# Hymba trunk layer: each pair's filled-in projections moved from ahead of the bonus products to ahead of the keys' transposes

## Chip, cores and metric

The kernel runs on one core of a Trainium2 chip. Its time is that of the device for one execution, in microseconds (us), and the median of several runs counts; lower is better. The core has a matrix engine (PE, whose weight loads the profile lists apart as PEld), a vector engine (DVE), a scalar engine (ACT), GpSimd (POOL) and a sync engine (SP) that issues most DMAs. Each works through its own instructions in order and waits at semaphores for the others. PE writes its products to PSUM, which has eight banks; ACT or DVE take them from there.

## What is computed

One layer of a hybrid decoder trunk for 512 prompt rows and 32 sample rows (8 requests of 4), all float32. Around the middle stand two half-step SwiGLU feed-forward parts with layer norms; in the middle a RWKV-7 recurrence of 8 heads of 64 runs beside a gated short convolution. Cut to what matters:

```python
x = layer_norm(ALPHA * x + 0.5 * swiglu(x, wg, wu, wd), ln1_g, ln1_b)
proj = x @ w_in                                   # r, k, v, decay, a, gate; conv columns
ps_mix = ps + mu_shift * (prev - ps)              # token shift of the RWKV columns
kk = normalize(k * k_k); k = k * (1 + (a - 1) * k_a)
def step(s, inp):                                 # per head, s is 64 x 64
    sa = einsum("bhij,bhj->bhi", s, -kk_t)
    s = s * w_t + sa (kk_t * a_t)^T + v_t k_t^T
    return s, einsum("bhij,bhj->bhi", s, r_t)
o = group_norm(o) + sum(r * k * r_k) * v          # the last term is the bonus
mix = concat(o * g, conv(c_b, c_c, c_h)) @ w_out
x = layer_norm(ALPHA * x + mix, ...); then the second SwiGLU and layer norm
```

## The kernel before, in words

All large weights are split into a high and a low part (`wsplit`: a copy on ACT, L135, and a subtraction on DVE, L136, about 1 us each for 128 x 1024), and each product is three matmuls (`mm3`, L152 to L154). The 544 rows are worked in two halves of 256 and 288 columns; a product of one half has eight input blocks, so 24 matmuls.

The recurrence is done in chunks of 64 steps. The 8 heads make four *pairs* of two; pairs 0 and 1 are group 0, pairs 2 and 3 group 1. The order by time is: scores of pairs 0 and 1 (about 424 to 456 us), elimination of group 0 (`elim`), its rounds, its recurrence and norm, then scores of pairs 2 and 3 (553 to 582), elimination and rounds of group 1, its recurrence, then the output projection and the second feed-forward part.

`Pair.scores` is the critical piece of work here. For one pair it makes:

- three groups of score products (L1057) for the 9 chunks and both heads. They go to five tiles `sm` and one tile `mm`, and DVE multiplies each by a mask into SC (L1060, six masks; the sixth reads the `mm` tile). Two DMAs write SC to DRAM (L1064), from where the elimination loads it.
- two groups of transposes, of chunks 0 to 4 and then 5 to 8: the keys (L1071 and, packed, L1050), which ACT copies to BK and BS (L1080, L1082; for pair 2's first group DVE, L1078), and the values (L1088, L1090, L1091), which ACT copies to UV and UP (L1096, L1099). The operand `bkb` of L1057 and L1071 holds the pair's derived keys.
- the bonus products (L1103, two, of 256 and 320 columns), which DVE multiplies with the values (L1104).

PSUM's eight banks are five tiles named `sm` (scores, transposes, bonus) and three named `mm` (background products and the sixth score tile), taken in turn. A new tile waits until the one that had the bank before has been read.

The background is a queue `bg` of generators: the projections of the next pairs and of the convolution, whose products are cut into *pieces* of six matmuls (two input blocks), which yield 658 for 256 columns and 738 for 288. `weave(key, crit)` runs the critical generator, and at each number that it yields it runs pieces worth that number times `FILL[key]`: 0.93 for pair 0, 1.832 for pair 1, 0.531 for pair 2 and 0.85 for pair 3. At least one piece runs at any number above zero. The last piece of a product yields only 300 or nothing, so that a further piece may follow.

Where the next pairs need it, derivations run on DVE between these: L996, L1027 to L1040 make the next pair's keys, L914 and L918 mix a projection's columns. `elim` (L1122 to L1131) is a chain of small DVE steps; its result goes through DRAM (L1132, L1133) and comes back by L1136 into DM, and the rounds start with L1166 on PE. In the recurrence PE's L1248 waits for L1240 on DVE.

The code gives the order in which work is offered; the scheduler of the language then writes each engine's row of instructions by what it takes to be ready, and can put an instruction ahead of or behind where the code has it. What stands in the rows is shown with the change.

Of the kernel before, what the change touches and what calls it, by code (L numbers as in the profile page):

```python
# [55 lines left out]
def R(par):  # L56
    return slice(64 * par, 64 * par + 64)
# [4 lines left out]
def body(ctx: ExitStack, tc: tile.TileContext, xT, gu1, wd1, win, wo_c, wo_0, wo_1, gu2, wd2, wl, ln3, eye, lora, vec, cst,  # L62
# [27 lines left out]
    def big():  # L90
        return ps.tile([P, 512], F32, name="mm", bufs=3)

    def sm():
        return ps.tile([P, 512], F32, name="sm", bufs=5)
# [795 lines left out]
    def s64(x):  # L890
        return x.rearrange("p (c t) -> p c t", t=64)
# [74 lines left out]
    class Pair:  # L966
# [75 lines left out]
        def scores(self):  # L1042
            p, pl, bkb, nk, vf = self.p, self.pl, self.bkb, self.nk, self.v

            def packed(qs, c0, src):
                for par, q in enumerate(qs):
                    for i, x in enumerate(src(par)):
                        if x is not None:
                            r0 = 64 * par + 32 * i
                            PE.matmul(q[r0:r0 + 32, c0:c0 + 64], x, ident[R(par), :], start=True, stop=True)  # L1050

            AR, bv = ARs[p // 2], bvs[p // 2]
            for a0c, n in ((0, 4), (4, 4), (8, 1)):
                qs = (sm(), sm() if n > 1 else big())
                for c in range(n):
                    for par, q in enumerate(qs):
                        PE.matmul(q[:, c * P:(c + 1) * P], bkb[R(par), a0c + c, par:par + 2, :], AR[R(par), pl, a0c + c, :, :],  # L1057
                                  start=True, stop=True)
                for par, q in enumerate(qs):
                    DVE.tensor_tensor(SC[:, pl, par, a0c:a0c + n, :], q[:, :P * n].rearrange("p (c t) -> p c t", c=n),  # L1060
                                      (msk if n > 1 else msks)[:, None, :].to_broadcast([P, n, P]), op=OP.mult)
                yield 0
            for par in range(2):
                dma(Ad[par].rearrange("(c d) s t -> d s c t", d=2)[pl, 0:64], SC[R(par), pl, par, 0:8, 0:64])  # L1064
            yield 500
            for a0c, n in ((0, 5), (5, 4)):
                qs = (sm(), sm())
                m = n - a0c // 5
                for c in range(m):
                    for par, q in enumerate(qs):  # L1070
                        PE.transpose(q[:, c * 64:(c + 1) * 64],  # L1071
                                     bkb[R(par), a0c + c, par:par + 2, :].rearrange("p s t -> p (s t)"), ident[R(par), :])
                if a0c:
                    packed(qs, 192, lambda par: (bkb[R(par), 8, 2 * par, 0:32], bkb[R(par), 8, 1, 0:32]))
                for par, q in enumerate(qs):
                    src, dst = s64(q[:, :64 * m]), BK[:, pl, par, a0c:a0c + m, :]
                    if p == 2 and not a0c:
                        DVE.tensor_copy(dst, src)  # L1078
                    else:
                        ACT.activation(dst, src, AF.Copy)  # L1080
                    if a0c:
                        ACT.activation(BS[R(par), pl, 64 * par:64 * par + 64], q[R(par), 192:256], AF.Copy)  # L1082
                qs = (sm(), sm())
                for c in range(n):
                    t = 64 * (a0c + c)
                    d = slice(c * 64, (c + 1) * 64)
                    if t:
                        PE.transpose(qs[0][:, d], vf[R(0), t - 64:t + 64], ident[R(0), :])  # L1088
                    else:
                        PE.matmul(qs[0][R(1), d], vf[R(0), t:t + 64], ident[R(0), :], start=True, stop=True)  # L1090
                    PE.transpose(qs[1][R(0), d], vf[R(1), t:t + 64], ident[R(1), :])  # L1091
                if a0c:
                    packed(qs, 256, lambda par: (None, vf[R(par), TP:TP + 32]))
                for par, q in enumerate(qs):
                    o = R(1 - par)
                    ACT.activation(UV[o, pl, par, a0c:a0c + n, :], s64(q[o, :64 * n]), AF.Copy)  # L1096
                    if a0c:
                        v = slice(64 * par + 32, 64 * par + 64)
                        ACT.activation(UP[v, pl, :], q[v, 256:320], AF.Copy)  # L1099
                yield 500  # L1100
            for t0, t1, _ in SEG:
                q = sm()
                PE.matmul(q[:, :t1 - t0], bo, nk[:, t0:t1], start=True, stop=True)  # L1103
                DVE.tensor_tensor(bv[pl][:, t0:t1], vf[:, t0:t1], q[:, :t1 - t0], op=OP.mult)  # L1104
# [664 lines left out]
```

## Time and profile before

| | |
|---|---|
| median of 3 runs | 1072.67 us (1072.48 to 1074.12) |
| the profiled execution | 1072.43 us, span 1070.7 us |
| mean granted clock of PE | 0.998 |
| busy: PE, DVE, ACT, POOL | 98%, 79%, 54%, 14% of the span |
| PE busy in 424 to 445 us | 20.65 of 21 us |
| PE busy in 565 to 582 us | 16.22 of 17 us |

A row of a timeline gives the start, the duration, the engine, the line of the kernel, the operation, what it writes and reads (tile names without numbers), its shape and how many such instructions the row stands for; in brackets how long the engine was idle before it, and which instruction released it. Consecutive matmuls overlap, so the durations of rows add up to more than the time between their starts; lengths are taken from start to start. A row of the view by stretches gives the stretch, its length, the busy time of PE, PEld, DVE, ACT and POOL with the number of instructions, the granted clock, the share of the DMA engines and GB/s. A row of the view of waits gives who waits for whom, with total us, number of times and the longest. A row of the DMA issues gives the number of transfers, the size of one and the median us from issue to landing.

### The profile page before, as it was taken

How to read it: one execution, taken by the hardware profiler on the slowest of the kernel's cores; microseconds unless marked ns; L12 is line 12 of the kernel's file. 1: busy time of each engine (PE TensorE's matmuls, PEld its weight loads, DVE VectorE, ACT ScalarE, POOL GpSimd, SP SyncE). 2: the span in 40 equal slices, each digit the busy share in tenths (PEclk: the TensorE clock that was granted, in tenths of full speed). 3: DMA queues.
4: the chain of work that ended last, by engine and by line, in shares of the span. 5: the costliest groups of instructions: out<-in, count | busy, mean ns of one | idle time of the engine just before them, and what ended most of it. 6: DMA issues, size and time to landing. Idle time of an engine off the chain costs nothing.

```text
span 1070.7 us, 22612 instructions
## 1 busy us (share of the span) xinstructions
PE 1050.7 (98%) x9178; PEld 1010.5 (94%) x9178; DVE 844.7 (79%) x1557; ACT 583.2 (54%) x1070; POOL 154.9 (14%) x273
## 2 busy tenths in 40 slices
PE   9999999999999999999999999999999999999997
PEld 8999999999999999899889988999999999999996
DVE  6797888979875777793578657988979888797757
ACT  5746555555553668654444435767555555555524
POOL 0111121211200022133101200001211212121000
PEclk9999999999999999999999999999999999999999
DMA  8558585676854233324145724434766848668512
GB/s 292 132 112 186 120 199 135 145 172 132 186 118 158 79 88 109 85 82 99 41 143 161 173 81 139 141 119 79 152 165 137 200 101 194 143 137 189 147 43 84
DMA packets 91528, 144.48 MB, mean 135 GB/s; under 512 B 34848, under 2 KB 52384, under 8 KB 91296
## 3 DMA queue, kind: packets, MB, share of 16 engines
q1 hardware_dynamic: 68144, 110.76, 34.2%
q0 software_dynamic: 22848, 31.72, 19.2%
q8 instruction: 72, 1.18, 0.4%
q10 hardware_dynamic: 432, 0.56, 0.2%
q14 instruction: 32, 0.26, 0.1%
HBM read 128.81 MB, written 9.75 MB: 129 GB/s over the span
## 4 chain that ended last, share of the span: by engine, by line
PE 76%; DVE 13%; ACT 7%; issue 2%; DMA 2%; POOL 0%; ACTq 0%; DVEq 0%; SPq 0%
PE mm L553 9%; PE mm L554 9%; PE mm L555 9%; PE sm L553 6%; PE sm L554 6%; PE sm L555 6%; PE mm L152 6%; PE mm L153 5%; PE mm L154 5%; DVE hhl L141 2%; ACT hl L135 2%; DVE hl L136 2%; PE sm L441 1%; PE sm L1166 1%; PE mm L784 1%
## 5 line engine op out<-in xcount | busy, mean ns | idle before, releaser
L136 DVE TENSOR_TENSOR hl<-raw,hl 128x1024 fp32r<-128x1024 f32 (+3 forms) x230 | 270.2, 1179 | 63.7 <-ACT hl L135 62.6
L135 ACT ACTIVATE hl<-raw 128x1024 fp32r<-128x1024 f32 (+3 forms) x230 | 232.9, 1020 | 69.7 <-DVE raw L519 43.5
L152 PE MATMUL mm<-xhl,hl 128*128 128x256 f32 (+1 forms) x704 | 209.2, 299 | 0.5 <-ACT xhl L140 0.5
L153 PE MATMUL mm<-xhl,hl 128*128 128x256 f32 (+1 forms) x704 | 203.0, 289 | 0.4 <-DVE xhl L141 0.4
L154 PE MATMUL mm<-xhl,hl 128*128 128x256 f32 (+1 forms) x704 | 202.0, 287 | 0.0
L152 PEld LDWEIGHTS mm<-xhl,hl 128*128 128x128 f32 x704 | 132.0, 188 | 6.9 <-issue 2.0
L153 PEld LDWEIGHTS mm<-xhl,hl 128*128 128x128 f32 x704 | 132.3, 188 | 2.7 <-issue 1.0
L154 PEld LDWEIGHTS mm<-xhl,hl 128*128 128x128 f32 x704 | 132.3, 188 | 0.3 <-issue 0.2
L555 PE MATMUL sm<-xhl,hl 128*128 128x272 f32 x432 | 125.2, 290 | 0.0
L554 PE MATMUL sm<-xhl,hl 128*128 128x272 f32 x432 | 124.4, 288 | 0.0
L553 PE MATMUL sm<-xhl,hl 128*128 128x272 f32 x432 | 124.1, 287 | 0.0
L553 PE MATMUL mm<-tv,hl 128*128 128x272 f32 x288 | 83.3, 289 | 0.3
L555 PE MATMUL mm<-tv,hl 128*128 128x272 f32 x288 | 83.4, 290 | 0.0
L554 PE MATMUL mm<-tv,hl 128*128 128x272 f32 x288 | 83.1, 288 | 0.0
L553 PEld LDWEIGHTS sm<-xhl,hl 128*128 128x128 f32 x432 | 81.4, 188 | 0.0
L554 PEld LDWEIGHTS sm<-xhl,hl 128*128 128x128 f32 x432 | 81.3, 188 | 0.0
L555 PEld LDWEIGHTS sm<-xhl,hl 128*128 128x128 f32 x432 | 81.2, 188 | 0.0
L532 POOL DMA_DIRECT2D raw<-in_wd x32 | 39.2, 1462 | 288.0 <-DVE hlb L141 225.2
L526 POOL DMA_DIRECT2D raw<-in_gu x36 | 43.3, 1203 | 203.5 <-DVE hlb L141 143.8
L553 PE MATMUL mm<-hhl,hl 128*128 128x272 f32 x192 | 56.4, 300 | 0.3
L554 PE MATMUL mm<-hhl,hl 128*128 128x272 f32 x192 | 55.9, 291 | 0.8 <-DVE hhl L141 0.2
L553 PEld LDWEIGHTS mm<-tv,hl 128*128 128x128 f32 x288 | 54.2, 188 | 1.9 <-ACT cpb L620 1.9
(416 smaller groups left out, 2716.0 us busy)
## 6 DMA issues: line engine op xcount, KB each, us to landing
raw<-in_gu SPq DMA_DIRECT2D x84, 512.0 KB, 4.5
raw<-in_gu POOLq DMA_DIRECT2D x36, 512.0 KB, 6.6
raw<-in_wd SPq DMA_DIRECT2D x32, 512.0 KB, 4.5
raw<-in_win SPq DMA_DIRECT2D x26, 512.0 KB, 3.6
raw<-in_wd POOLq DMA_DIRECT2D x32, 256.0 KB, 6.0
z<-sv POOLq DMA_DIRECT2D x16, 272.0 KB, 8.4
raw<-in_wo_c SPq DMA_DIRECT2D x8, 512.0 KB, 3.6
raw<-in_wd SPq DMA_DIRECT2D x8, 384.0 KB, 3.2
```

Of the source, the lines that this page charges most:

```text
L135: seen["hi"] = ACT.activation(hl[:, 0, a:b], raw[:, a:b], AF.Copy)
L136: seen["lo"] = DVE.tensor_tensor(hl[:, 1, a:b], raw[:, a:b], hl[:, 0, a:b].bitcast(F32), op=OP.subtract)
L141: return DVE.tensor_tensor(lo, x, hi.bitcast(F32), op=OP.subtract)
L152: PE.matmul(out, wh, src[:, 0, k, c0:c1], start=(start and i == 0), stop=False)
L153: PE.matmul(out, wh, src[:, 1, k, c0:c1], start=False, stop=False)
L154: seen["fill"] = PE.matmul(out, wl, src[:, 0, k, c0:c1], start=False, stop=(stop and i == n - 1))
L441: PE.matmul(o[i][h][:, :c1 - c0], block(hl, v, k), xhl[:, y, k, c0:c1], start=(k == 0 and j == 0), stop=(k == KD - 1 and j == 2), skip_gro ...
L526: POOL.dma_start(x.rearrange("p (s c) -> p s c", s=2), bass.AP(tensor=a11.tensor, offset=a11.offset, ap=[[2 * D, P], [P * 2 * D, 2], [1, 5 ...
L532: POOL.dma_start(four(x)[:, i], bass.AP(tensor=a11.tensor, offset=a11.offset, ap=[[DFF, P], [P * DFF, 2], [1, 256]]), accum_op=OP.add)
L553: PE.matmul(out, wh, src(0, i), start=(first and i == 0), stop=False, skip_group_check=True)
L554: PE.matmul(out, wh, src(1, i), start=False, stop=False, skip_group_check=True)
L555: PE.matmul(out, wl, src(0, i), start=False, stop=(i == n - 1), skip_group_check=True)
```

## The change

Two yields of `Pair.scores` get other numbers. The one behind the masks yields 1000 instead of 500, and the one at the end of the second group of transposes 0 instead of 500; the one at the end of the first group stays 500.

```diff
             for par in range(2):
                 dma(Ad[par].rearrange("(c d) s t -> d s c t", d=2)[pl, 0:64], SC[R(par), pl, par, 0:8, 0:64])
-            yield 500
+            yield 1000
             for a0c, n in ((0, 5), (5, 4)):
...
-                yield 500
+                yield 0 if a0c else 500
             for t0, t1, _ in SEG:
                 q = sm()
                 PE.matmul(q[:, :t1 - t0], bo, nk[:, t0:t1], start=True, stop=True)
```

In pieces of background (ahead of the key transposes, between the two groups, ahead of the bonus products): pair 0 has 1, 1, 2 before and 2, 2, 0 after; pair 1 has 2, 2, 2 and 4, 2, 0; pair 2 has 1, 1, 1 and 1, 1, 0; pair 3 has half a piece, 2, 1 and two, 2, 0. What is not run there runs behind the bonus products or has run already.

The first place is PE in pair 0, from the sixth score product (to `mm_5067`) to the first key transpose. Before, with `mm_5035` as the background product:

```order
L1057 MATMUL mm_5067<-AR0_4714,bkb_4806 128x128 [waits Activation_49]
L152 MATMUL mm_5035<-xhl_68,hl_5005 128x288
L153 MATMUL mm_5035<-xhl_68,hl_5005 128x288
L154 MATMUL mm_5035<-xhl_68,hl_5005 128x288
...
L1071 MATMUL sm_5080<-cs_4701,bkb_4806 128x64 [waits DVE_49]
L1071 MATMUL sm_5081<-cs_4701,bkb_4806 128x64 [waits DVE_49]
```

There are six matmuls of `mm_5035` between these. After the change twelve stand there, and ahead of the bonus products, where six of 288 and six of 256 columns stood, now none does; the last rows of the second group of transposes (a packed value block) are followed at once by L1103:

```order
L1088 MATMUL sm_5149<-cs_4701,v_4303 128x64 [waits Pool_49]
L1091 MATMUL sm_5150<-cs_4701,v_4303 64x64
L1050 MATMUL sm_5149<-cs_4701,v_4303 32x64
L1050 MATMUL sm_5150<-cs_4701,v_4303 32x64
L1103 MATMUL sm_5165<-nk_4805,cs_4701 128x256 [waits Activation_49]
L1103 MATMUL sm_5168<-nk_4805,cs_4701 128x320 [waits PE_49,Activation_49]
```

What moved is the background between the last transposes and L1103.

The second place is PE in pair 1, the key transposes of the first group. Before, the ten stand together behind twelve matmuls of `mm_5276`, and the next background, `mm_5368`, follows the values:

```order
L154 MATMUL mm_5276<-xhl_68,hl_5272 128x256
L1071 MATMUL sm_5340<-cs_4701,bkb_5172 128x64 [waits DVE_49]
L1071 MATMUL sm_5341<-cs_4701,bkb_5172 128x64 [waits DVE_49]
...
L1091 MATMUL sm_5355<-cs_4701,v_4303 64x64
L152 MATMUL mm_5368<-xhl_68,hl_5272 128x288 [waits DVE_49]
L153 MATMUL mm_5368<-xhl_68,hl_5272 128x288
```

After the change:

```order
L154 MATMUL mm_5276<-xhl_68,hl_5272 128x256
L1071 MATMUL sm_5353<-cs_4701,bkb_5172 128x64 [waits DVE_49]
L1071 MATMUL sm_5354<-cs_4701,bkb_5172 128x64 [waits DVE_49]
...
L1071 MATMUL sm_5353<-cs_4701,bkb_5172 128x64
L152 MATMUL mm_5340<-xhl_68,hl_5272 128x288 [waits DVE_49]
L153 MATMUL mm_5340<-xhl_68,hl_5272 128x288
...
L154 MATMUL mm_5340<-xhl_68,hl_5272 128x288
L1071 MATMUL sm_5354<-cs_4701,bkb_5172 128x64
L1071 MATMUL sm_5353<-cs_4701,bkb_5172 128x64
```

Twelve matmuls of `mm_5340`, which waits for DVE, now stand behind the fifth of the ten key transposes; the other five, the values and twelve more matmuls of the same product follow. The instruction of DVE that its wait names is the sixth mask, whose tile had the same bank.

The third place is DVE in pair 3, around the six masks. Before:

```order
L918 SCALAR_TENSOR_TENSOR T12_4300<-pb_7002,vc_66,dt_7003 128x32
L136 TENSOR_TENSOR hl_7335<-raw_7334,hl_7335 128x1024 [waits DMAHW7_49,PE_49,Activation_49]
L1060 TENSOR_TENSOR SC_4703<-sm_7031,cs_4701 128x512 [waits PE_49]
L1060 TENSOR_TENSOR SC_4703<-sm_7032,cs_4701 128x512 [waits PE_49]
L1060 TENSOR_TENSOR SC_4703<-sm_7043,cs_4701 128x512 [waits PE_49]
L1060 TENSOR_TENSOR SC_4703<-sm_7044,cs_4701 128x512 [waits PE_49]
```

After the change:

```order
L918 SCALAR_TENSOR_TENSOR T12_4300<-pb_6995,vc_66,dt_6996 128x32
L136 TENSOR_TENSOR hl_7204<-raw_7203,hl_7204 128x1024 [waits DMAHW0_49,PE_49,Activation_49]
L1060 TENSOR_TENSOR SC_4703<-sm_7025,cs_4701 128x512 [waits PE_49]
L1060 TENSOR_TENSOR SC_4703<-sm_7026,cs_4701 128x512 [waits PE_49]
L136 TENSOR_TENSOR hl_7339<-raw_7338,hl_7339 128x1024 [waits DMAHW7_49,Activation_49]
L1060 TENSOR_TENSOR SC_4703<-sm_7037,cs_4701 128x512 [waits PE_49]
L1060 TENSOR_TENSOR SC_4703<-sm_7038,cs_4701 128x512 [waits PE_49]
```

A second split of a weight stands between the second and the third mask. The split that came first before stood earlier, in pair 3's derivation (between L1027 and L1028, at 563.59 us in the profile), and has moved out of it to ahead of the masks. Elsewhere on DVE a few splits, L914 and steps of the eliminations change places.

## The prediction

> **What bounds the kernel now.** I read the first part of the page, to see which engine sets the pace:
>
> ```profile
> span 1070.7 us, 22612 instructions
> ...
> PE 1050.7 (98%) x9178; PEld 1010.5 (94%) x9178; DVE 844.7 (79%) x1557; ACT 583.2 (54%) x1070; POOL 154.9 (14%) x273
> ```
>
> PE is busy for 1050.7 of 1070.7 us, so 20 us in all are PE's idle time. The change takes no matmul away and adds none. It can gain only idle time of PE around the four scores stages, and lose by making new idle time there or in what depends on them. So I asked for PE's waits from the first scores stage to the second output projection (424 to 680 us):
>
> ```profile
> PE sm L1248 <- DVE UV L1240: 3.4, 8, 0.7
> ...
> PE sm L1091 <- DVE SC L1060: 0.8, 3, 0.3
> PE sm L1071 <- DVE SC L1060: 0.7, 2, 0.3
> ```
>
> The columns are total us, times, longest. The longest, 3.4 us, lie in the recurrence behind the scores (L1248). For the masks (L1060 on DVE) PE waits 1.5 us in five places: the key transposes (L1071) and value transposes (L1091) need PSUM banks that the masks still read. That is what more background products ahead of the key transposes can cover. How dense the stage is shows the view by stretches of time, for pair 1:
>
> ```profile
> 445.00:458.00 13.00, 12.20 (x131) 10.69 (x128) 9.22 (x16) 10.62 (x25) 1.55 (x10) 1.00 0.33 73
> ```
>
> PE is busy 12.20 of 13 us at a granted clock of 1.00: 0.8 us idle is all there is to win here.
>
> **Pair 0.** The PE timeline (start, duration, line, count, and in brackets idle time with its releaser):
>
> ```profile
> 427.87 0.40 PE L152 MATMUL mm<-xhl,hl 128*128 128x288 f32 x1
> ...
> 428.86 0.54 PE L1071 MATMUL sm<-cs,bkb 64*128 64x64 f32 x10
> 429.47 0.33 PE L1090 MATMUL sm<-cs,v 64*64 64x64 f32 x2
> 430.07 0.24 PE L1091 MATMUL sm<-cs,v 64*64 64x64 f32 x1 [0.28 <-DVE SC L1060]
> ...
> 430.47 0.40 PE L152 MATMUL mm<-xhl,hl 128*128 128x288 f32 x1
> ...
> 434.26 1.13 PE L1103 MATMUL sm<-nk,cs 128*128 128x256 f32 x4
> ```
>
> One piece of background (six matmuls of 288 columns) takes 428.86 - 427.87 = 0.99 us ahead of the first group of transposes. The group then takes 1.61 us to the next piece, part of it waiting for the fourth mask. After the change two pieces stand ahead, two between the groups and none ahead of the bonus products. I need three lengths that this stage doesn't show undisturbed, and take them from pair 1:
>
> ```profile
> 448.81 0.52 PE L1071 MATMUL sm<-cs,bkb 64*128 64x64 f32 x9 [0.33 <-DVE SC L1060]
> ...
> 450.40 0.40 PE L152 MATMUL mm<-xhl,hl 128*128 128x288 f32 x1
> ...
> 452.19 0.40 PE L1071 MATMUL sm<-cs,bkb 64*128 64x64 f32 x6
> ...
> 453.39 0.40 PE L152 MATMUL mm<-xhl,hl 128*128 128x288 f32 x1
> ...
> 455.08 1.13 PE L1103 MATMUL sm<-nk,cs 128*128 128x256 f32 x4
> ```
>
> Twelve matmuls of 288 columns take 452.19 - 450.40 = 1.79 us up to the transposes; the second group of transposes 453.39 - 452.19 = 1.20 us. Six of 256 with six of 288 take 1.68 (pair 3's rows below, 575.23 to 576.91).
>
> After the change, then: background from 427.87, transposes at 427.87 + 1.79 = 429.66. The fourth mask let L1091 start at 430.07, so almost nothing is left to wait for: ten key transposes are 0.54 busy, and from the first L1091 to the next piece it is 430.47 - 430.07 = 0.40, together 0.94. The next piece starts at 430.60, the second group at 432.28, the bonus products (L1103) at 433.48 instead of 434.26: **0.78 us gained**. If only the marked wait of 0.28 goes, group 1 takes 1.61 - 0.28 = 1.33 and the gain is 0.39; I take 0.78, since the masks are done by then, and keep 0.39 as the other end. Below nothing it can't be, since the masks end when they did and PE has the same work. What follows of pair 0 (the derivation of pair 1's keys on DVE) starts earlier too: the same weight split moves ahead of the first bonus product's L1104 on DVE and costs nothing there, since L1104 waits for L1103.
>
> **Pair 1, the place that costs.** Here a yield is worth more background: two pieces stood ahead of the transposes, and four do now. The scheduler writes the first two of these (mm_5276), then five of the ten key transposes, then the other two pieces (mm_5340), and then the other five transposes. The pieces of mm_5340 write a PSUM bank that the sixth mask still reads. Before the change the same bank was first written by the piece at 450.40, behind all the first group. The sixth mask, on DVE:
>
> ```profile
> 450.06 0.28 DVE L1060 TENSOR_TENSOR SC<-mm,cs 128x128 f32<-128x128 f32 x1
> ```
>
> It ends at 450.34; the piece at 450.40 came 0.06 behind it. With everything 0.78 earlier it ends at 449.56 and the pieces start at 449.62. PE, in order, has nothing else meanwhile: the five transposes and the values, which used to fill this wait, now stand behind the pieces. From there: 1.79 for twelve matmuls, 451.41; five transposes (half of 0.52) with the values (0.40) and the change of operands between them, about 0.75, 452.16; twelve matmuls, 453.95; second group, 455.15 for L1103. Without the change in pair 1 it would be 455.08 - 0.78 = 454.30. So **0.85 us lost**, and pair 1 leaves PE 0.07 late. The ends: if the masks don't come earlier with pair 0 (DVE's chain on its own), the loss counts from 450.34 and the stage ends 0.86 late instead of 0.07. If the pieces need not wait, they start behind the five transposes: the second mask lets these run from 448.81 - 0.78 = 448.03, so the pieces from 448.29, and L1103 comes 1.79 + 0.75 + 1.79 + 1.20 later, at 453.82, a gain of 0.48 on 454.30 instead of a loss.
>
> [...]
>
> **Pairs 2 and 3.** Here a yield is worth one piece. In pair 2 the piece ahead of L1103 moves behind it: bonus products and pair 3's derivation start 0.9 to 1.0 earlier, and nine matmuls of 256 fewer stand ahead of pair 3's score products: 0.133 - (1.79 - 1.68)/6 = 0.115 each, 1.0 us. Pair 3's rows, PE and DVE:
>
> ```profile
> 570.10 2.14 PE L1057 MATMUL sm<-AR,bkb 64*128 64x128 f32 x33
> ...
> 575.23 0.38 PE L152 MATMUL mm<-xhl,hl 128*128 128x256 f32 x1
> ...
> 576.91 0.40 PE L1071 MATMUL sm<-cs,bkb 64*128 64x64 f32 x6
> ...
> 579.01 1.13 PE L1103 MATMUL sm<-nk,cs 128*128 128x256 f32 x4
> ```
>
> ```profile
> 571.16 1.22 DVE L136 TENSOR_TENSOR hl<-raw,hl 128x1024 fp32r<-128x1024 f32 x1
> 572.30 2.68 DVE L1060 TENSOR_TENSOR SC<-sm,cs 128x512 f32<-128x512 f32 x5
> ```
>
> The scores start at about 569.0, so the masks could start 1.1 earlier or more. But between the second and the third mask DVE now makes another weight split, which holds it for 572.30 - 571.16 = 1.14 us. Laid behind one another, DVE's rows put masks one and two about 1.36 earlier (one split less ahead of them, 1.14, and 0.22 that the earlier bonus products bring), three to six only 0.22: the fourth lets L1091 start 0.22 us earlier, and the background behind it starts at 575.01 instead of 575.23. The last piece moves behind L1103 and joins the background there, which saves one start behind small products: the first matmul of a piece costs about 0.1 more than those inside (six take 0.99 alone, twelve 1.79, not 1.98). **0.33 us gained**; ends: nothing (the masks stay where they are) and 0.6 (one PE wait at L1071 and one at L1091 gone, 0.3 each).
>
> **Sum.** -0.78 + 0.85 - 0.33 = -0.26 us. Behind the scores PE is as full as elsewhere, so a shift of PE arrives at the end. The profiled execution took 1072.43 us (span 1070.7 and 1.7 around it), which gives 1072.17. The median of the three runs, 1072.67, is 0.24 above it, and the same difference gives **1072.4**. With all ends on the good side it is -0.78 - 0.48 - 0.6 = -1.86, on the bad side +0.86 (pair 1's masks not earlier, nothing in pair 3). A measurement of this kernel can tell about 0.2%, 2.1 us, from no change; the forecast lies far inside.
>
> **What else hangs on the moved steps.** ACT evacuates the second group later or earlier with PE, and no bank is wanted sooner than it is freed: in pair 0 ACT now takes the copy of a weight split before that group, and by the order of the rows ends it about when the group ends on PE. The masked scores go through DRAM: two loads of DM follow the eliminations of group 1, and the chunk products wait for them:
>
> ```profile
> 597.77 1.32 SPq L1136 DMA_DIRECT2D DM<-Dd  x2
> ```
>
> ```profile
> DM<-Dd SPq DMA_DIRECT2D x2, 256.0 KB, 6.1
> ```
>
> ```profile
> 606.27 2.08 PE L1166 MATMUL sm<-DM,SC 64*64 64x64 f32 x64
> ```
>
> The second load is issued half of 1.32 after 597.77 and lands 6.1 us later, at about 604.5; its first user starts at 606.27, so 1.8 us of lateness are covered. The scheduler writes pair 2's and 3's splits in other places of DVE's row, and I expect the elimination to end up to 0.7 us later and at most one split, 1.22. Both lie below 1.8, so I cost it at nothing. SP's queue passes one weight load behind the two Dd writes, which only helps them. In group 0 the elimination's last steps move ahead of a weight split and of the convolution's work on DVE, so its load can only be earlier.
>
> **Rivals.**
> 1. The pieces of pair 1 don't stall PE, because the sixth mask comes earlier or frees the bank in time. Then pair 1 gains 0.48: -0.78 - 0.48 - 0.33 = -1.59, 1071.1, still within 0.2%. Against it: the mask ended 0.06 before the row at 450.40, and DVE has a split, a scan and the five other masks ahead of it in the same order as now. Chance 0.11.
> 2. Slower: group 1's elimination. The two splits beside pair 3's masks and those moved in the elimination add up, DM lands late, and PE runs out of background ahead of L1166. It decides from 1.8 us of lateness on, each us beyond costs one, and slower by over 0.2% needs 1.8 + 2.1 + 0.3 = 4.2 us, three and a half splits: 1074.8 or so. For it: DVE is busy 79% and in order. Against it: the number of splits in the stretch is the same. Chance 0.13.
> 3. The stall in pair 1 lowers the clock. [...] Nothing in the rows shows a clock below 1.00 here. Chance 0.04.
> 4. The change does nothing: PE's pieces move but each gain is a wait elsewhere, 1072.7. Chance 0.05.
> 5. Faster: DVE's new order in group 0 lets the elimination and the splits end earlier, and of the 3.4 us that PE waits at L1248 two thirds go, because a split or copy no longer stands ahead of L1240: -0.26 - 2.2, 1070.2. For it: the order on DVE does change there. Against it: these waits sit in a chain of PE and DVE that the change leaves as it is. Chance 0.09.
>
> **How the numbers follow.** The forecast, 1070.8 to 1073.5 by its ends, has 0.58. Same is 0.58 + 0.11 + 0.05 = 0.74, faster 0.09 (rival 5), slower 0.17 (rivals 2 and 3). The range goes from 1070.5, short of rival 5, to 1074.6, into rival 2 and short of rival 3; it leaves out 0.04 + 0.09 and a part of rival 2, under 0.2 together.
>
> **What would show it.** Right: in pair 0 no PE wait at L1091, and L1103 about 5.6 us behind the first background matmul (433.48 - 427.87), not 6.4; in pair 1 a wait at L152 of 1 us or more whose releaser is DVE SC L1060, between two rows of five L1071; in pair 3 a split between the second and third mask, and L1091 still released by a mask; PEclk at 9 throughout. Wrong: no wait at L152 in pair 1 (rival 1); a wait at L1166 for DM (rival 2); a clock below 1.00 (rival 3); or PE waits in the recurrence that grow by more than the terms above.

## The result, and the profile after

The changed kernel takes 1075.21 us (median of 17 runs, 1072.77 to 1076.7), the kernel before 1072.54 (17 runs, 1071.69 to 1074.25). The ratio is 1.0018, 95% interval 1.0012 to 1.0025: slower by 1.9 us by the ratio and by 2.7 by the medians, clear of the noise though small. The forecast was that nothing measurable would change, and the time lies outside the stated range of 1070.5 to 1074.6. The profiled execution took 1076.37 us, 3.94 more than that of before.

The page of the changed kernel:

```profile
span 1074.6 us, 22614 instructions
...
PE 1054.8 (98%) x9178; PEld 1014.0 (94%) x9178; DVE 844.2 (79%) x1557; ACT 582.4 (54%) x1070; POOL 154.4 (14%) x273
...
PEclk9999999999999999899999999999999999999999
```

PE is busy 4.1 us longer for the same 9178 matmuls. So on balance the time did not go into waits: the same work ran slower, and one slice of PEclk, the seventeenth (430 to 457 us), shows an 8. The waits of PE between 424 and 680 us:

```profile
PE sm L1248 <- DVE UV L1240: 3.4, 8, 0.7
PE mm L152 <- DVE SC L1060: 1.3, 1, 1.3
PE sm L1239 <- ACT W L1233: 0.9, 3, 0.4
PE sm L1090 <- DVE SC L1060: 0.9, 1, 0.9
```

The second row is the stall that was predicted, a background matmul (L152) that waits for a mask, once, 1.3 us. The fourth is new as well and was not predicted. The recurrence's waits (first row) are what they were. Pair 1 on PE:

```profile
448.45 0.34 PE L1071 MATMUL sm<-cs,bkb 64*128 64x64 f32 x4 [0.33 <-DVE SC L1060]
450.04 0.40 PE L152 MATMUL mm<-xhl,hl 128*128 128x288 f32 x1 [1.25 <-DVE SC L1060]
...
450.67 0.29 PE L153 MATMUL mm<-xhl,hl 128*128 128x288 f32 x1
450.80 0.35 PE L154 MATMUL mm<-xhl,hl 128*128 128x288 f32 x1
450.95 0.44 PE L152 MATMUL mm<-xhl,hl 128*128 128x288 f32 x1
451.19 0.44 PE L153 MATMUL mm<-xhl,hl 128*128 128x288 f32 x1
```

The stall ends at 450.04. The matmuls behind it start 0.13 apart, as before; from 450.95 on they start 0.24 apart and last 0.44 instead of 0.29. In the view by stretches (the column behind POOL's is the granted clock) the clock is lower in just this time:

```profile
450.00:451.00 1.00, 0.96 (x7) 0.96 (x8) 0.38 (x1) 0.00 (x0) 0.56 (x4) 0.95 0.68 179
451.00:457.00 6.00, 6.00 (x35) 5.32 (x34) 1.37 (x2) 1.63 (x4) 0.00 (x0) 0.50 0.36 49
457.00:458.00 1.00, 1.00 (x16) 0.55 (x14) 0.00 (x0) 0.56 (x3) 0.11 (x1) 0.63 0.00 0
```

For 0.10 + 6 + 0.74 = 6.84 us the granted clock is 0.50. That is rival 3 of the prediction, the one with a chance of 0.04.

### The profile page after: what moved, and what is told of

The parts are those of the page before. It is cut to its first block, busy times and chain, and to the rows that moved or that the text cites. A ratio compares the mean times of both kernels' runs of the same rounds, so it can differ in the third digit from the quotient of the medians.

```text
span 1074.6 us, 22614 instructions
## 1 busy us (share of the span) xinstructions
PE 1054.8 (98%) x9178; PEld 1014.0 (94%) x9178; DVE 844.2 (79%) x1557; ACT 582.4 (54%) x1070; POOL 154.4 (14%) x273
## 4 chain that ended last, share of the span: by engine, by line
PE 80%; DVE 11%; ACT 5%; DMA 2%; issue 2%; ACTq 0%; DVEq 0%; SPq 0%
PE mm L553 9%; PE mm L554 9%; PE mm L555 9%; PE mm L152 7%; PE mm L153 6%; PE mm L154 6%; PE sm L553 6%; PE sm L554 6%; PE sm L555 6%; DVE hhl L141 2%; ACT hl L135 2%; PE sm L441 1%; DVE hl L136 1%; PE sm L1166 1%; PE mm L784 1%
## 5 line engine op out<-in xcount | busy, mean ns | idle before, releaser
L152 PE MATMUL mm<-xhl,hl 128*128 128x256 f32 (+1 forms) x704 | 209.9, 300 | 1.8 <-DVE SC L1060 1.3
L152 PEld LDWEIGHTS mm<-xhl,hl 128*128 128x128 f32 x704 | 132.7, 189 | 8.0 <-issue 2.2
```

What stands on the lines that cost most here:

```text
L152: PE.matmul(out, wh, src[:, 0, k, c0:c1], start=(start and i == 0), stop=False)
```

## The experiments

The theory made from this, A: PE's idle time in pair 1 lets the granted clock fall (0.50 for 6.84 us in the profile), and that is most of the loss. The rival, B: the new order itself costs the time (transposes behind four pieces, masks behind a split), and the clock only goes along. A kernel's runs and the runs of before stand on the same chip. Each run gives a mean granted clock, and times of one kernel go with it: of the changed kernel's 17 runs the four at 0.999 took 1072.77 to 1073.69, the eight at 0.995 or 0.996 took 1075.79 to 1076.7. A mean of 0.998 alone does not mean that the clock fell during the work: it also drops behind the last matmul, to 0.50 at 1065.81 us in the profile of the kernel before and at 1072.13 in that of the changed one, and the first of these has 0.998 for that reason alone.

**The change without pair 1.**

```diff
-            yield 1000
+            yield 500 if p == 1 else 1000
...
-                yield 0 if a0c else 500
+                yield 0 if a0c and p != 1 else 500
```

> The change for pairs 0, 2 and 3, with pair 1's two yields as they were before. Theory A (the clock): what cost the time is PE's idle time of 1.25 us in pair 1 behind the fifth key transpose, which lets the granted clock fall to half for some 6.7 us. Without that idle time no row shows a clock below 0.9, pair 0 keeps its gain of 0.3 to 0.8, pairs 2 and 3 come out within 0.3 of nothing, and the time is 1071.6 to 1072.5, a ratio of 0.999 to 1.000 to the kernel before. Theory B (the order): the loss is in the later masks and transposes themselves, in pair 3 as much as in pair 1, and the clock only goes along. Then about half of the loss stays: 1073.5 to 1074.5, ratio 1.001 to 1.002.

Measured: 1072.57 us, ratio 0.9997 (0.9988 to 1.0006), clock in 445 to 462 us 1.00. The loss is gone with pair 1's part, although pair 3's does all it did in the changed kernel (a wait of 0.9 us at L1090 there). A's ratio came in (its time lies 0.07 above A's upper end), B's didn't.

**The change for pair 1 alone.**

```diff
-            yield 500
+            yield 1000 if p == 1 else 500
...
-                yield 500
+                yield 0 if a0c and p == 1 else 500
```

> The change for pair 1 alone; pairs 0, 2 and 3 yield as before. Theory A: the wait for the sixth mask at the first background matmul behind the fifth transpose is there again, 1.2 to 1.6 us, the granted clock falls to half in some runs behind it, and the median is 1075 to 1077, ratio 1.0025 to 1.004, with single runs near 1073.3 in which the clock did not fall or fell for a shorter time. Theory B: pair 1 alone costs the 0.85 us of the prediction's term and no more, 1073.4, ratio 1.001, with little spread.

Measured: 1075.06 us (1073.46 to 1076.89), ratio 1.0020 (1.0011 to 1.0028). Pair 1 alone gives a loss as large as the whole change. A's median came in, its ratio (1.0025 to 1.004) was too high; B's number and its little spread did not come in. The profiled execution of this kernel took 1073.69 us; it shows the same stall without a fall of the clock, which separates the two:

```profile
448.84 0.34 PE L1071 MATMUL sm<-cs,bkb 64*128 64x64 f32 x4 [0.33 <-DVE SC L1060]
450.44 0.41 PE L152 MATMUL mm<-xhl,hl 128*128 128x288 f32 x1 [1.25 <-DVE SC L1060]
...
452.23 0.40 PE L1071 MATMUL sm<-cs,bkb 64*128 64x64 f32 x5
```

```profile
445.00:462.00 17.00, 15.29 (x150) 13.41 (x147) 12.36 (x29) 11.50 (x27) 1.93 (x12) 1.00 0.27 57
```

The wait is 1.25 us in both. Here twelve matmuls take 452.23 - 450.44 = 1.79 us, in the changed kernel's profile 452.52 - 450.04 = 2.48, and the next twelve 3.17 (454.10 to 457.27). From the stall's end to L1103 it is 5.76 here (to 456.20) and 8.62 there (to 458.66): the fall of the clock cost 2.86 us of PE's time. What the stall and its order cost without a fall is worked out below.

**The stall filled with work.** The changed kernel, with pair 1's larger yield in two halves and repeated transposes between them, which write the same values to the first transposes' tiles:

```diff
+            if p == 1:
+                yield 500
+                first = (sm(), sm())
+                for i in range(28):
+                    q = first[i % 2]
+                    PE.transpose(q[:, 0:64], bkb[R(i % 2), 0, i % 2:i % 2 + 2, :]..., ident[R(i % 2), :])
-            yield 1000
+            yield 500 if p == 1 else 1000
             for a0c, n in ((0, 5), (5, 4)):
-                qs = (sm(), sm())
+                qs, first = first or (sm(), sm()), None
```

> The changed kernel, but in pair 1 twenty-eight repeated transposes (the same result written to the first two tiles of the transposes again and again) stand behind the first two pieces of background, where PE waited for the sixth mask; all ten key transposes then follow the background. The wait for the mask is as long as in the changed kernel, but PE works through most of it; the work behind it is 0.26 us longer. Theory A: the clock stays at 1.00 in this stretch and the time falls to 1072.2 to 1073.2, ratio 0.9995 to 1.0006. Theory B: the transposes and the background come as late as in the changed kernel, so the time stays at 1075 to 1076.5.

And the same with `range(10)`:

> As the run with twenty-eight repeated transposes in pair 1, but with ten: PE works for 0.5 us less... about 0.9 us less of the wait for the sixth mask, so that some 1.3 to 1.4 us of idle time is left there, about that of the changed kernel. Theory A with a sharp limit on idle time (the clock falls where PE is idle for over 1.2 us or so within 3.4 us): the clock falls in more than half the runs and the median is 1074.5 to 1076. Theory A with a gradual chance: some runs at 1073 to 1074, some at 1075 and over, median 1074 to 1075. Theory B (no clock): 1073.8 as with twenty-eight, since the work behind the mask is the same.

Measured: with 28 repeats 1073.79 us (1073.03 to 1075.38), ratio 1.0008 (1.0000 to 1.0017); with 10 repeats 1076.41 us (1074.16 to 1083.45), ratio 1.0039 (1.0024 to 1.0054). PE's rows at the stall, with 28:

```profile
448.28 1.09 PE L1071 MATMUL sm<-cs,bkb 64*128 64x64 f32 x27 [0.33 <-DVE SC L1060]
449.88 0.40 PE L152 MATMUL mm<-xhl,hl 128*128 128x288 f32 x1 [0.50 <-DVE SC L1060]
```

With 10:

```profile
448.22 0.52 PE L1071 MATMUL sm<-cs,bkb 64*128 64x64 f32 x9 [0.33 <-DVE SC L1060]
...
449.81 0.40 PE L152 MATMUL mm<-xhl,hl 128*128 128x288 f32 x1 [1.07 <-DVE SC L1060]
```

The two kernels differ in 18 transposes whose result is thrown away. The background starts at the same time within 0.1 us, and the kernel with *more* work for PE is faster by 2.6 us in the median. The two ran on different chips; their ratios to the kernel before, each taken on one chip, differ by 0.0031, some 3.3 us. The clocks of the runs with 28 are 0.997 to 0.999, those with 10 are 0.990 to 0.999. B has no account of that. A's number for 28 repeats was too low by 0.6 us: PE still waits 0.50 for the mask and 0.5 once at L995, for ACT, and neither stands in it. A's two medians for 10 repeats (1074 to 1075 and 1074.5 to 1076) were too low as well. With ten repeats PE has less idle time in pair 1 than in the changed kernel (1.52 us in the worst 3.4, against 1.71), and yet the loss is larger. So the size of the idle time in pair 1 does not by itself set the loss, and that the 18 transposes help by filling this one stall is not shown: the only profile with ten repeats that shows a fall, below, has it at pair 2.

**Second profiles.** The changed kernel once more, and the one with ten repeats once more, no edits:

> The changed kernel once more, for a second profile. If the fall of the clock is a matter of where PE's idle 1.25 us lies against a window that runs on its own, this profile shows either the same wait with the clock at 1.00 and a time of 1073 or so, or the same wait with the clock at 0.5 for some 3.4 or 6.7 us and 1074.7 or 1076.4: steps of about 1.7 us. If the fall belongs to the wait itself, it is the same as in the first profile, 6.7 us.

> The run with ten repeated transposes once more, for a profile. Its times reach from 1074.2 to 1083.5 at mean clocks from 0.999 to 0.990, and the one profile shows no fall. If the spread is the clock's, a profile at 1075.5 or above shows the clock at 0.5 in one or several stretches of about 3.4 us, which begin within 3.4 us behind the waits of pair 1 or pair 3; a profile near 1074.2 shows none. If it were something else, a profile at 1075.5 or more would show the clock at 1.00 and longer waits or loads.

The changed kernel took 1076.01 us, with the clock down in two places:

```profile
450.00:451.00 1.00, 1.00 (x8) 1.00 (x7) 0.00 (x0) 0.00 (x0) 0.21 (x2) 0.60 0.90 195
451.00:453.00 2.00, 2.00 (x14) 1.49 (x13) 1.37 (x2) 0.41 (x2) 0.00 (x0) 0.50 0.16 20
453.00:454.00 1.00, 1.00 (x12) 0.83 (x12) 0.00 (x0) 0.65 (x3) 0.00 (x0) 0.69 1.11 104
...
518.00:519.00 1.00, 1.00 (x11) 0.93 (x8) 0.76 (x4) 0.43 (x2) 0.00 (x0) 0.73 0.00 0
519.00:521.00 2.00, 2.00 (x12) 2.00 (x11) 0.43 (x2) 0.00 (x0) 0.00 (x0) 0.50 0.00 0
521.00:522.00 1.00, 1.00 (x7) 0.78 (x6) 0.00 (x0) 0.00 (x0) 0.00 (x0) 0.56 0.00 0
```

The first is 0.80 + 2 + 0.62 = 3.42 us at half clock behind the stall, the second 0.54 + 2 + 0.88 = 3.42 us in the recurrence of group 0. The first profile's 6.84 is twice that. The kernel with ten repeats took 1079.36 us, and its fall lies at pair 2:

```profile
555.00:559.00 4.00, 2.81 (x37) 2.31 (x37) 3.26 (x6) 1.27 (x3) 0.00 (x0) 1.00 0.38 83
559.00:560.00 1.00, 1.00 (x7) 1.00 (x6) 1.00 (x3) 0.00 (x0) 0.00 (x0) 0.71 0.88 357
560.00:569.00 9.00, 9.00 (x65) 6.90 (x65) 3.98 (x10) 2.92 (x10) 0.00 (x0) 0.50 0.19 46
569.00:570.00 1.00, 1.00 (x8) 1.00 (x8) 0.97 (x2) 0.00 (x0) 0.00 (x0) 0.67 0.00 0
```

0.58 + 9 + 0.66 = 10.24 us, three times 3.41, and the run is 5.2 us above the profile of the same kernel without a fall (1074.16), about half of 10.24. So the falls measured in these three profiles last 3.42, 6.84 and 10.24 us, one, two and three times 3.41, and the same stall is followed by none (pair 1 alone), by 3.42 us or by 6.84. The expectation that a fall begins within 3.4 us behind a wait of pair 1 or 3 failed for that last one, which follows 4 us in which PE is idle for 1.19, in one wait for DVE at pair 2's score products.

The traces also show in what the like stalls differ. The changes of the granted clock named here lie whole numbers of stretches of 3.413 us apart, called windows below and laid in each trace from the first entry of its clock. In the changed kernel this entry is at 7.18 us, and the fall (450.91), the rise (457.74) and the fall behind the last matmul (1072.13) come 130, 132 and 312 windows behind it; in the kernel before it is at 4.27, and the one fall, at 1065.81, comes 311 windows behind it. In the second profile of the changed kernel the falls at 450.20, 518.46 and, behind the last matmul, 1071.42 lie 20 and 162 windows apart. The first entry comes at another time in each of the two traces, so the same stall lies differently on the windows. These are the windows with pair 1's waits: one of the changed kernel, one of its second profile, and two of the run with pair 1 alone:

```profile
447.50:450.91 3.41, 1.70 (x13) 1.23 (x13) 2.88 (x7) 1.85 (x5) 1.04 (x7) 1.00 0.63 182
446.79:450.20 3.41, 1.70 (x14) 1.23 (x13) 3.01 (x7) 1.98 (x5) 1.03 (x7) 1.00 0.64 180
445.82:449.23 3.41, 2.91 (x30) 2.30 (x26) 3.40 (x5) 3.35 (x6) 0.34 (x2) 1.00 0.18 24
449.23:452.64 3.41, 2.21 (x18) 1.97 (x19) 2.11 (x6) 0.58 (x3) 0.71 (x5) 1.00 0.68 207
```

Twice both waits, 0.33 and 1.25 us, lie in one window, PE is idle for 1.71 us of it, and the clock falls at its end. With pair 1 alone a border of windows lies between the two waits, the windows have 0.50 and 1.20 us idle, and no fall follows. What sets the clock these three profiles do not show.

Idle time alone does not order the falls, though. A window with 1.33 us idle (ten repeats, first profile, 447.96 to 451.37) is followed by no fall, the one with 1.19 ahead of pair 2's by the longest. The window ahead of the fall in the recurrence above has no idle time at all:

```profile
515.05:518.47 3.42, 3.42 (x103) 3.27 (x98) 0.74 (x3) 1.31 (x6) 0.57 (x2) 1.00 0.53 158
```

**The cause of the stall taken away.** The score products of the last chunk are made first:

```diff
-            for a0c, n in ((0, 4), (4, 4), (8, 1)):
+            for a0c, n in ((8, 1), (0, 4), (4, 4)):
```

Their two masks, 0.27 and 0.28 us, then free the `mm` bank before the four large ones. With the changed yields:

> The changed kernel, with the score products of the last chunk first: groups (8,1), (0,4), (4,4) in place of (0,4), (4,4), (8,1). The two small masks then come first on DVE, 0.28 us each, and the bank of the sixth score tile is free some 2 us earlier; the transposes wait for a small mask and the first three large ones instead of the four large ones. Theory A: no wait for a mask at L152 in pair 1, clock 1.00, and the gain of the prediction's first rival (1.6 us) with perhaps 0.5 more for the other pairs: 1070.3 to 1071.3, ratio 0.998 to 0.999. Theory B: the transposes of pair 1 still stand behind four pieces of background, and pair 3's masks behind the second split: 1072.5 to 1074.

Measured: 1071.84 us (1071.28 to 1073.83), ratio 0.9989 (0.9980 to 0.9997), faster than the kernel before by 0.1%, just clear of the noise, and so faster than the changed kernel. B's number did not come in. In pair 1 PE has no idle time left, and the clock stays:

```profile
445.00:462.00 17.00, 17.00 (x160) 15.60 (x157) 12.35 (x33) 11.36 (x28) 2.14 (x13) 1.00 0.32 74
```

The time is still 0.5 above the upper end of A's expectation; PE's waits in this kernel name two that it didn't count, one at the next pair's L995 and one in pair 3:

```profile
PE sm L1091 <- DVE SC L1060: 1.1, 1, 1.1
PE sm L995 <- ACT kq L989: 0.9, 1, 0.9
```

With the yields of before:

> The kernel before (its yields 500 and 500), with the score products of the last chunk first, as in the run with that order and the changed yields. It tells what of that run's gain is the order's and what the yields'. Theory A (the new yields are worth 0.6 us in pair 0 and the wait in pair 1 costs 1 us and the clock; both waits are for masks): with small masks first the waits for masks at L1071 and L1091 shrink from 1.5 to under 0.6 us and the time is 1071.7 to 1072.4, ratio 0.9985 to 0.9995, so that the changed yields still bring 0.3 to 0.6 beside it. Theory B (the order does it all, the yields nothing): 1071.8 or less, as with the changed yields.

Measured: 1072.20 us, ratio 0.9992 (0.9983 to 1.0001). A's number came in, B's didn't, but the interval reaches just past 1, so that the order alone gains is not shown, and the 0.4 us to the kernel with the changed yields lies inside both intervals. The profiled execution, 1073.14 us, shows a granted clock of 0.51 over 516.0 to 519.4 us, in the recurrence: falls are not the change's alone.

With the changed yields for fewer pairs, group 0 only and all but pair 3:

> Small score products first, the changed yields for pairs 0 and 1 only; pairs 2 and 3 yield as before. In the run with all pairs changed, PE waits 1.1 us at L1091 in pair 3, where the third and fourth mask stand behind a weight split. Theory A: that wait is the rest of the loss; without the changed yields there one split stands ahead of the four large masks instead of between them, PE's wait is shorter and the time is 1070.8 to 1071.6, ratio 0.998 to 0.9988, with no run above 1073.5. Theory B: the masks behind the split cost the same wherever it stands: 1071.6 to 1072.2.

> Small score products first, the changed yields for pairs 0, 1 and 2, pair 3 as before: can it beat the run in which all four pairs are changed (1071.84)? One theory: the wait of 1.1 us at L1091 in pair 3 comes from the second weight split between the masks, which stays in this order of DVE, so the time is the same within 0.3: 1071.5 to 1072.2. The rival: it comes from pair 3's own larger yield, which is gone here: 1070.8 to 1071.4.

Measured: 1072.84 us, ratio 0.9995 (0.9986 to 1.0003), and 1073.92 us, ratio 1.0009 (1.0001 to 1.0018). Both missed their expectations. The first can't be told from the other two small-first kernels. The second tells something: its profile, at a clock of 0.999, took 1071.93 us, about as the kernel with all pairs changed, but eight of its 12 runs took 1073.51 to 1076.34 at clocks of 0.995 to 0.998. PE waits there once, in pair 3,

```profile
PE sm L1091 <- DVE SC L1060: 1.2, 1, 1.2
```

0.1 us longer than with all pairs changed, where only one run of 11 came above 1073. That a tenth of a microsecond decides it is not shown, nor that this wait brings falls: no profile of this kernel shows where its clock falls in such a run.

## Why the prediction was wrong

The step that failed is the one on the clock: the sum takes the stall at its own length and has no term for a lower clock. The stall itself came where and as it was predicted (1.25 us, released by the sixth mask, between two rows of five key transposes). In both profiles of the changed kernel the granted clock went to 0.50 within a microsecond behind it, for 6.84 and 3.42 us; in the first this cost 2.86 us of PE's time. The rows of before do not show what a stall of 1.25 us does: in them waits of at most 0.3 us at the masks go with a granted clock of 1.00. Summed over 3.4 us PE is idle 0.80 us in pair 1 before the change and 1.71 after; 0.80 is the most in any such stretch of the four scores stages of before. Rival 3, a lower clock behind the stall, stands in the sum of the chances with 0.04 and above the upper end of the range. No run behind the prediction shows that term, neither how far the clock falls behind a stall nor for how long; in its place both profiles showed 0.50 for the times above, and eight of the 17 runs have mean clocks of 0.996 or less.

By the terms, in the first profile:

- **Pair 0**, predicted 0.78 gained: the first score product starts 0.16 later than before (425.82, noise ahead of the change), L1103 0.45 earlier, so 0.61 was gained, between the two ends given (0.39 and 0.78).

```profile
429.81 0.52 PE L1071 MATMUL sm<-cs,bkb 64*128 64x64 f32 x10
430.27 0.32 PE L1090 MATMUL sm<-cs,v 64*64 64x64 f32 x2
430.52 0.24 PE L1091 MATMUL sm<-cs,v 64*64 64x64 f32 x1
```

No wait stands here, as forecast, but from the first transpose to L1091 it is 0.71, not the 0.54 of the sum, which had left the change from keys to values out.
- **Pair 1**, predicted 0.85 lost: at full clock (pair 1 alone) the scores start 0.04 later than before and L1103 comes 1.12 later, so 1.08 lost. The second half of the first group took 0.97 (452.23 to 453.20) instead of 0.75. Then the clock: 2.86 more.
- **Pairs 2 and 3**, predicted 0.33 gained: from pair 2's first transpose to the 256-column background behind pair 3's scores the lag to before grows from 3.54 to 3.59, so nothing. DVE in pair 3:

```profile
573.60 1.22 DVE L136 TENSOR_TENSOR hl<-raw,hl 128x1024 fp32r<-128x1024 f32 x1
574.74 1.28 DVE L1060 TENSOR_TENSOR SC<-sm,cs 128x512 f32<-128x512 f32 x2
575.93 1.22 DVE L136 TENSOR_TENSOR hl<-raw,hl 128x1024 fp32r<-128x1024 f32 x1
577.07 1.48 DVE L1060 TENSOR_TENSOR SC<-sm,cs 128x512 f32<-128x512 f32 x3
```

The split stands between the masks as the order said, but the masks are 0.25 later than reckoned: one of the elimination's L1122 (0.69 us, at 566.45) had moved into the derivation in place of the split, and the sum left it out. So L1090 waits 0.88 and L1091 0.28, and PE stands where it stood.
- **The elimination** (rival 2): L1166 starts 3.60 later than before, the same lag as ahead of it, so it cost nothing, as forecast.

At full clock these sum to -0.61 + 1.08 + 0.05 = +0.52 instead of -0.26, inside 0.2%, and the changed kernel's runs at a mean clock of 0.999, 1072.77 to 1073.69, are that case: a mean of 0.999 leaves no room for a fall of 3.4 us. They lie inside the stated range, though the predicted gain is not in them; the median belongs to the others. With the fall, +0.52 + 2.86 = 3.38 of the profile's 3.94; 0.16 lies ahead of the change, and the last 0.4, nearly all of it behind the scores, is not explained.

Left open: what makes the clock fall. Idle time alone does not order the falls, as the windows above show. Whether the kind of work matters, such as the small matmuls of the recurrence and of the transposes, no run here tests: none varies it with the idle time fixed. Why a fall lasted one, two or three windows is open too.

## What to carry to other kernels

The stall of PE in pair 1 had two prices here: its own length, 1.25 us, and, in both profiles of the changed kernel, a granted clock of 0.50 for one or two stretches of 3.4 us behind it. Each such stretch cost 1.4 to 1.7 us (2.86 for two, and 5.2 for the three at pair 2 with ten repeats). A window in which PE was idle for 1.71 of 3.41 us was followed by a fall in both profiles that show one; of three windows with 1.19, 1.20 and 1.33 us idle the first was and the others weren't, so no limit is known from these runs. So when work is moved ahead of a wait, look in the order for what the moved work itself waits for (here a PSUM bank whose reader, the sixth mask, stood last), and free that first. And read PEclk and the mean clock of every run beside the waits: here PE was busy 4.1 us longer with the same 9178 matmuls, and the clock was at 0.50 for 6.84 us.

## What the runs showed that was not expected

- Granted clock 0.50 for 3.42, 6.84 and 10.24 us in single profiles, behind windows of 3.413 us in which PE was idle for 1.71 us, for 1.19 or not at all; in another profile with the same stall none.
- The kernel before seems to have such falls as well, in some runs: its times spread from 1071.69 to 1075.35, and beside the experiments all of its runs of 1073.5 and above have mean clocks of 0.996 to 0.998. Its one profile shows none ahead of its last matmul; that of the kernel with its yields and the small score products first does.
- With 28 transposes of no use placed in a wait the kernel is 2.6 us faster in the median than with 10 of them (ratios 1.0008 and 1.0039 to the kernel before).
